# The sample group's bias in DRAM: twelve stores of shifted rows and six loads, in place of one store and 56 loads

## The chip, the cores and the metric

One Trainium2 chip, one core. The metric is the device time of one execution in microseconds (us). Engines are called PE (TensorE), DVE (VectorE), ACT (ScalarE), POOL (GpSimd) and SP (SyncE, which here only issues DMAs); ACT and POOL also issue some. L706 is line 706 of the kernel before.

## The reference

One inference step of one decoder layer, all in float32, for two groups of tokens that share the weights: a prompt of 2048 tokens, and a sample group of 8 sequences with 4 new tokens each and a cache of 1024 past positions. The input is normed and projected into three branches: attention over dilated windows (12 heads), a causal depthwise convolution, and cross-attention into 256 memory rows. What the change touches is the attention of the sample group: each head evaluates three patterns, and to each score a bias from a shared table is added that depends on head, pattern and distance.

```python
PATTERNS = ((128, 1), (512, 4), (2048, 16))   # window, dilation

def _dilated_gather(q, k_all, v_all, bias, d, nw, wb, past):
    i = jnp.arange(T)[:, None]
    j = jnp.arange(nw + 1)[None, :]
    kpos = past + i - j * d                    # keys at distances 0, d, .. nw*d
    ...
    s = jnp.einsum('bthd,btjhd->bthj', q, kg).astype(jnp.float32)
    s = s + bias.astype(jnp.float32)
    s = jnp.where(valid[None, :, None, :], s, NEG)
```

The four new tokens of a sequence stand one position apart, so along a row of cached keys the bias of token t is that of its neighbour, moved by one place.

## The kernel before, in words

The work stands in one long program. First (`phase_a1`) x is normed, transposed and split into a high and a low half, and multiplied with the columns of w_in block by block (u, q, k, v, qc); every float32 product is three matmuls, hi*hi, hi*lo and lo*hi (`gemm`, L166 to L168). The convolution of each u block follows on DVE. Then, in `build`, come `memory` (memory keys and values, the norm of the convolution's output, cross-attention), `sample_bias`, `sample_attention` and `attention`, and last `phase_c` with the output products. Beside memory and both attentions runs a generator of further column blocks (`sweep`: za, zb, zc, gt; tiles gg, weights whi and wlo), which gives TensorE work between the others.

The program's text isn't the order on the engines. The framework orders the instructions when the context closes, by a simulated timeline (`schedule_with_timeline_sim=True`): each engine and queue gets a list in which an instruction may move ahead of others that are not ready by that simulation. On the chip each engine then goes through its own list strictly in order. So loads of a later function can come early: those of `sample_bias` stand among those of `memory`.

The bias goes through DRAM:

- `bias_rows`, early in `phase_a1`, makes `exs`, 12 partitions (a head each) by 3 patterns by 752, with six small matmuls (L377) and six copies (L378) on DVE, and stores it to `d_exs` (L379). Row p of a head holds the negated bias over shifted positions: 515 places for the last 512 cached keys, 7 for the new ones, 4 x 32 for the older keys that only pattern 2 reaches, and one row's blocks are moved by 32 for a token.
- Behind it `blk_u` loads `st_in`, the old convolution rows (L275), which TensorE transposes (L279).
- `sample_bias` builds three tiles, one a pattern, of 112 rows: rows 0 to 47 and 64 to 111 are head times 4 plus token, twice. A memset fills a tile (L696, L698), then for each of the two halves and each of the four tokens one load brings 512 places (L706), one the 4 new places (L707), and for pattern 2 one the 128 older places (L709). Each load writes 12 partitions, four apart, from a place in `d_exs` that moves with the token. A copy (L710) repeats the new places eight times. That is 3 x 2 x 4 x 2 + 8 = 56 loads, all issued by SP.
- `sample_attention` reads the three tiles, some 400 us later, for its scores.

Other names that the prediction uses, all at the start of `memory`: `c` are chunks of the convolution's output (load L663), whose norm goes through DVE (L665, L668, L673, L685), ACT (sq, L671 and L684), POOL (L681) and two small matmuls (str L667, sco L675); `mt` are the memory rows (L913), `msq` their squares on ACT (L915), `mrs` and `mrr` the factors of their norm (L64 to L68); `wraw` from w_mem_kv are the memory weights (L150), which POOL splits into whi (L55) and wlo (L56).

Of the kernel before, what the change touches and what calls it, by code (L numbers as in the profile page):

```python
# [7 lines left out]
F32 = mybir.dt.float32  # L8
# [11 lines left out]
HA, DA, EA = 12, 64, 768  # L20
# [3 lines left out]
NT_S = 752  # L24
# [13 lines left out]
class K:  # L38
# [316 lines left out]
    def bias_rows(self, cpool, pool, psum):  # L355
        nc, I = self.nc, self.I
        rb = self.rb = cpool.tile([33, HA], F32, name="rb")
        nc.vector.memset(rb, 1.0e30)
        raw = pool.tile([32, HA], F32, name="rbr")
        nc.sync.dma_start(raw, I["rel_bias"])  # L360
        nc.vector.tensor_scalar(rb[0:32], raw, -1.0, None, op0=ALU.mult)
        oh = pool.tile([33, 3, 384], F32, name="oh")
        nc.sync.dma_start(oh, I["c_onehot"])
        ext = pool.tile([HA, 3, 384], F32, name="ext")
        for p in range(3):
            t = psum.tile([128, 512], F32, name="tr")
            nc.tensor.matmul(t[:HA, :384], rb, oh[:, p, :], start=True, stop=True)
            nc.vector.tensor_copy(ext[:, p, :], t[:HA, :384])
        nc.sync.dma_start(self.d_ext, ext)
        ohs = pool.tile([33, 3, NT_S], F32, name="ohs")  # L370
        nc.sync.dma_start(ohs, I["c_onehot_s"])
        exs = pool.tile([HA, 3, NT_S], F32, name="exs")
        for p in range(3):
            for c in range(0, NT_S, NT_S // 2):
                cs = slice(c, c + NT_S // 2)
                t = psum.tile([128, 512], F32, name="tr")
                nc.tensor.matmul(t[:HA, :NT_S // 2], rb, ohs[:, p, cs], start=True, stop=True)  # L377
                nc.vector.tensor_copy(exs[:, p, cs], t[:HA, :NT_S // 2])  # L378
        nc.sync.dma_start(self.d_exs, exs)  # L379
        pf = pool.tile([128, 3, 128], F32, name="permf")  # L380
        nc.sync.dma_start(pf, I["c_perm"])
        self.perm = cpool.tile([128, 3, 128], R32, name="perm")
        nc.vector.tensor_copy(self.perm, pf)
# [305 lines left out]
    def sample_bias(self, keep):  # L689

        nc = self.nc
        NK, R = 672, 112
        self.sbias = []
        for p in range(3):
            bt = keep.tile([R, NK], F32, name=f"sb{p}")
            nc.vector.memset(bt, 1.0e30 if p < 2 else 0.0)  # L696
            nw = keep.tile([R, 4], F32, name=f"sn{p}")
            nc.vector.memset(nw, 0.0)  # L698
            base = self.d_exs[:, p, :]
            for r in (0, 64):  # L700
                for t in range(4):
                    rows = slice(r + t, r + 48, 4)

                    def src(o, n):
                        return bass.AP(tensor=base.tensor, offset=base.offset + o, ap=[[base.ap[0][0], HA], [1, n]])
                    nc.sync.dma_start(bt[rows, 0:512], src(3 - t, 512))  # L706
                    nc.sync.dma_start(nw[rows, :], src(515 + 3 - t, 4))  # L707
                    if p == 2:
                        nc.sync.dma_start(bt[rows, 512:640], src(522 + 32 * (3 - t), 128))  # L709
            nc.vector.tensor_copy(bt[:, 640:NK].rearrange("p (b t) -> p b t", t=4), nw[:, None, :].to_broadcast([R, 8, 4]))  # L710
            self.sbias.append(bt)


    def sample_attention(self):
# [505 lines left out]
    def scratch(self, dp):  # L1220
        t = lambda n, sh: dp.tile(sh, F32, name=n)
        self.d_q = [t(f"d_q{j}", [128, T]) for j in range(6)]
        self.d_k = [t(f"d_k{j}", [128, T]) for j in range(6)]
        self.d_qc = [t(f"d_qc{j}", [128, T]) for j in range(4)]
        self.d_za = [t(f"d_za{j}", [128, T]) for j in range(6)]
        self.d_zb = [t(f"d_zb{j}", [128, T]) for j in range(6)]
        self.d_zc = [t(f"d_zc{j}", [128, T]) for j in range(4)]
        self.d_c = t("d_c", [6, 128, T])
        self.d_actb = t("d_actb", [6, 128, T])
        self.d_ext = t("d_ext", [HA, 3, 384])  # L1230
        self.d_exs = t("d_exs", [HA, 3, NT_S])
        self.d_st = [t(f"d_st{h}", [6, S]) for h in range(HA)]
        self.d_cf = [t(f"d_cf{j}", [3, 2 * S]) for j in range(6)]
        self.d_act = [None if 6 <= j < 12 else t(f"d_act{j}", [128, T]) for j in range(16)]
        self.d_act[6:12] = [self.d_actb[j] for j in range(6)]
        self.d_g = [t(f"d_g{j}", [128, T]) for j in range(24)]
        self.d_x = [None] + [[[t(f"d_x{th}{c}{k}", [128, THIRDS[th][1]]) for k in range(8)] for c in range(2)]
                             for th in (1, 2)]
# [69 lines left out]
```

## Time and profile before

| | before |
|---|---|
| median of 3 runs | 3151.36 us (3148.8 to 3155.62) |
| profiled execution | 3154.4 us |
| its span | 3152.6 us |
| PE busy | 3000.2 us, 95% of the span |
| DVE busy | 2014.8 us, 64% |
| POOL busy | 1350.4 us, 43% |
| ACT busy | 1124.2 us, 36% |
| DMA | 454.66 MB, mean 144 GB/s |
| chain that ended last | PE 70%, DMA 12%, DVE 7%, issue 4%, POOL 3%, ACT 2%, SP's queue 1% |

The profile is of one execution. Its busy times are sums over the span; a row of a timeline gives start, length, engine, line, operation, what is written from what, and in brackets how long the engine had idled before and what released it. A queue such as SPq only issues transfers: its rows are the time of the issue, and the transfer lands later. The chain follows each instruction back to what released it; "issue" in it is time without a wait that the profile shows.

### The profile page before, as it was taken

The numbers are of one execution on the slowest core, as the hardware profiler recorded it, in microseconds if no ns is written. First come the engines' busy times: TensorE is split into PE (matmuls) and PEld (weight loads), VectorE is DVE, ScalarE is ACT, GpSimd is POOL, SyncE is SP. The second block draws the span as 40 slices with busy tenths as digits, with TensorE's granted clock in tenths as the row PEclk, the third lists the DMA queues.
The fourth block names the chain that finished last, engine by engine and source line by source line (L and its number), as shares of the span: only waits on it lengthen the run. The fifth ranks groups of instructions, "written<-read, shape, count | busy, mean of one in ns | idle before, by whom it ended". The sixth has DMA issues, their size and how long they took to land.

```text
span 3152.6 us, 55374 instructions
## 1 busy us (share of the span) xinstructions
PE 3000.2 (95%) x20705; PEld 2839.9 (90%) x20705; DVE 2014.8 (64%) x3734; ACT 1124.2 (36%) x2835; POOL 1350.4 (43%) x1048
## 2 busy tenths in 40 slices
PE   7999999999987999999999999989899979999998
PEld 6899999999987999998999999989898967787897
DVE  5297797796677926465546766666656457556563
ACT  5010010010132433243437575656565523222221
POOL 0121221142356537444256565667676433233240
PEclk9899999999999999999999999999999989999999
DMA  7232222211265454477454656576555487657561
GB/s 250 85 103 80 80 60 61 63 62 50 81 182 167 135 153 144 147 219 239 151 139 116 161 123 163 128 185 150 156 143 152 109 279 227 223 168 227 161 197 53
DMA packets 532218, 454.66 MB, mean 144 GB/s; under 512 B 118191, under 2 KB 458581, under 8 KB 531137
## 3 DMA queue, kind: packets, MB, share of 16 engines
q1 hardware_dynamic: 357502, 335.36, 36.2%
q10 hardware_dynamic: 169840, 105.02, 11.7%
q0 software_dynamic: 4608, 10.75, 1.2%
q8 instruction: 164, 2.69, 0.4%
q14 instruction: 104, 0.85, 0.1%
HBM read 332.96 MB, written 118.04 MB: 143 GB/s over the span
## 4 chain that ended last, share of the span: by engine, by line
PE 70%; DMA 12%; DVE 7%; issue 4%; POOL 3%; ACT 2%; SPq 1%; ACTq 0%; DVEq 0%; POOLq 0%
PE g L166 8%; PE g L167 8%; PE g L168 8%; PE gg L166 6%; PE gg L168 6%; PE gg L167 6%; PE pg L168 3%; PE pg L166 3%; PE pg L167 3%; PE pt L571 2%; DMA cb<-d_cf 2%; PE y L1180 2%; PE y L1179 2%; PE y L1178 2%; PE o L598 1%
## 5 line engine op out<-in xcount | busy, mean ns | idle before, releaser
L166 PE MATMUL gg<-x0h,whi 128*128 128x256 f32 (+1 forms) x2560 | 747.9, 292 | 25.9 <-DVE st L246 12.2
L168 PE MATMUL gg<-x0h,wlo 128*128 128x256 f32 (+1 forms) x2560 | 741.8, 290 | 0.1
L167 PE MATMUL gg<-x0l,whi 128*128 128x256 f32 (+1 forms) x2560 | 741.1, 290 | 0.0
L55 POOL TENSOR_SCALAR whi<-wraw 128x1024 fp32r<-128x1024 f32 x162 | 242.7, 1500 | 928.5 <-PE g L167 524.1
L166 PEld LDWEIGHTS gg<-x0h,whi 128*128 128x128 f32 x2560 | 493.2, 193 | 35.0 <-DVE st L246 13.7
L167 PEld LDWEIGHTS gg<-x0l,whi 128*128 128x128 f32 x2560 | 493.5, 193 | 2.2 <-issue 0.5
L168 PEld LDWEIGHTS gg<-x0h,wlo 128*128 128x128 f32 x2560 | 493.2, 193 | 2.2 <-POOL wlo L56 0.3
L322 DVE SCALAR_TENSOR_TENSOR acc<-G,cw,acc 128x1536 f32<-128x1536 f32 (+15 forms) x354 | 480.8, 1408 | 0.3
L56 POOL TENSOR_TENSOR wlo<-wraw,whi 128x1024 fp32r<-128x1024 f32 x162 | 417.0, 2575 | 9.4 <-PE gg L168 0.2
L155 POOL TENSOR_TENSOR clo<-craw,chi 128x768 fp32r<-128x768 f32 (+1 forms) x96 | 174.1, 1815 | 346.0 <-ACT chi L154 329.8
L627 ACT ACTIVATE P<-T,stm 128x128 f32<-128x128 f32 (+1 forms) x576 | 260.8, 455 | 141.0 <-DVE stm L625 94.8
L239 ACT ACTIVATE st<-g 128x384 f32<-128x384 f32 (+1 forms) x132 | 60.2, 461 | 570.7 <-PE g L168 550.7
L166 PE MATMUL pg<-ac,chi 128*128 128x512 f32 (+1 forms) x640 | 229.4, 359 | 16.6 <-ACT chi L154 8.7
L625 DVE CUSTOM_DVE_ANT_0 T<-s,bias 128x128 f32<-128x128 f32 (+1 forms) x576 | 191.5, 357 | 80.8 <-PE s L617 47.0
L167 PE MATMUL pg<-ac,chi 128*128 128x512 f32 (+1 forms) x640 | 228.8, 358 | 6.3 <-DVE ac L1198 6.3
L168 PE MATMUL pg<-ac,clo 128*128 128x512 f32 (+1 forms) x640 | 227.6, 357 | 3.6 <-POOL clo L155 3.6
L576 DVE TENSOR_TENSOR pl<-pt,ph 128x512 fp32r<-128x512 f32 x240 | 155.6, 652 | 52.4 <-ACT ph L575 48.9
L168 PE MATMUL g<-x0h,wlo 128*128 128x384 f32 x544 | 184.3, 339 | 2.9 <-POOL wlo L56 2.9
L166 PE MATMUL g<-x0h,whi 128*128 128x384 f32 x544 | 183.6, 338 | 2.6 <-ACT st L239 2.3
L167 PE MATMUL g<-x1l,whi 128*128 128x384 f32 x544 | 186.0, 342 | 0.0
L167 PE MATMUL g<-x0l,whi 128*128 128x384 f32 x544 | 185.8, 342 | 0.0
L168 PE MATMUL g<-x1h,wlo 128*128 128x384 f32 x544 | 185.8, 342 | 0.0
(330 smaller groups left out, 7425.0 us busy)
## 6 DMA issues: line engine op xcount, KB each, us to landing
wraw<-in_w_in ACTq DMA_DIRECT2D x119, 512.0 KB
d_g<-st ACTq DMA_DIRECT2D x168, 128.0 KB
cb<-d_cf SPq DMA_DIRECT2D x72, 256.0 KB
g<-d_g SPq DMA_DIRECT2D x72, 256.0 KB
wraw<-in_w_in SPq DMA_DIRECT2D x35, 512.0 KB
kvc<-in_cache_k_win SPq DMA_DIRECT2D x8, 1536.0 KB
kvc<-in_cache_v_win SPq DMA_DIRECT2D x8, 1536.0 KB
raw<-d_q SPq DMA_DIRECT2D x48, 256.0 KB
```

Source lines behind the costliest of these rows:

```text
L55: nc.gpsimd.tensor_scalar(hi, raw, 1.0, 1.0, op0=ALU.mult, op1=ALU.mult)
L56: nc.gpsimd.tensor_sub(lo, raw, hi.bitcast(F32))
L155: nc.gpsimd.tensor_sub(lo, raw, hi.bitcast(F32))
L166: nc.tensor.matmul(ps, hi[:, k, :], h, start=k == 0, stop=False)
L167: nc.tensor.matmul(ps, hi[:, k, :], l, start=False, stop=False)
L168: nc.tensor.matmul(ps, lo[:, k, :], h, start=False, stop=k == kb - 1)
L322: nc.vector.scalar_tensor_tensor(a3[:, lo:hi], G[:, src:src + hi - lo, 2 - m:130 - m], w, a3[:, lo:hi], op0=ALU.mult, op1=ALU.add)
L571: nc.tensor.transpose(t[:, 128 * x:128 * x + 128], pc, self.ident)
L576: nc.vector.tensor_tensor(pl[:, :w], t[:, :w], ph[:, :w].bitcast(F32), op=ALU.subtract)
L625: nc.vector.tensor_tensor_reduce(sc[:, :w], t[:, o:o + w], bias[:, 256 - w:256], 1.0, 3.0e38, ALU.add, ALU.min, m)
L627: nc.scalar.activation(P[:, o:o + w], sc[:, :w], AF.Exp, bias=m, scale=-1.0, accum_out=self.stl[:, col:col + 1])
L1178: nc.tensor.matmul(y[:m, c, :], ah[:, ts_], bh[:, cs], start=k == 0, stop=False)
```

## The change

`d_exs` gets a row for each head and token: 12 x 4 x 3 x 644 in place of 12 x 3 x 752. `bias_rows` stores each token's shifted piece, three stores a token, twelve in all, the same `exs` being read at four offsets. `sample_bias` has one tile of 112 x 3 x 672 in place of three of 112 x 672; head and token together are now 48 neighbouring rows in DRAM, so that one load for each half brings the 512 places of all three patterns, one the 128 older places and one the new ones: six loads. Three memsets stand for six; the three copies of the new places stay, now behind all loads in the program's text.

```diff
-        nc.sync.dma_start(self.d_exs, exs)
+        for t in range(4):
+            nc.sync.dma_start(self.d_exs[:, t, :, 0:512], exs[:, :, 3 - t:515 - t])
+            nc.sync.dma_start(self.d_exs[:, t, :, 512:516], exs[:, :, 518 - t:522 - t])
+            nc.sync.dma_start(self.d_exs[:, t, 2, 516:644], exs[:, 2, 522 + 32 * (3 - t):650 + 32 * (3 - t)])
...
-        self.sbias = []
+        bt = keep.tile([R, 3, NK], F32, name="sb")
+        nc.vector.memset(bt[:, 0:2], 1.0e30)
+        nc.vector.memset(bt[:, 2], 0.0)
+        nw = keep.tile([R, 3, 4], F32, name="sn")
+        nc.vector.memset(nw, 0.0)
+        src = self.d_exs.rearrange("h t p x -> (h t) p x")
+        for r in (0, 64):
+            nc.sync.dma_start(bt[r:r + 48, :, 0:512], src[:, :, 0:512])
+            nc.sync.dma_start(bt[r:r + 48, 2, 512:640], src[:, 2, 516:644])
+            nc.sync.dma_start(nw[r:r + 48], src[:, :, 512:516])
         for p in range(3):
-            bt = keep.tile([R, NK], F32, name=f"sb{p}")
-            nc.vector.memset(bt, 1.0e30 if p < 2 else 0.0)
-            nw = keep.tile([R, 4], F32, name=f"sn{p}")
-            nc.vector.memset(nw, 0.0)
-            base = self.d_exs[:, p, :]
-            for r in (0, 64):
-                for t in range(4):
-                    ...
-            nc.vector.tensor_copy(bt[:, 640:NK].rearrange("p (b t) -> p b t", t=4), nw[:, None, :].to_broadcast([R, 8, 4]))
-            self.sbias.append(bt)
+            nc.vector.tensor_copy(bt[:, p, 640:NK].rearrange("p (b t) -> p b t", t=4),
+                                  nw[:, p, None, :].to_broadcast([R, 8, 4]))
+        self.sbias = [bt[:, p] for p in range(3)]
...
-        self.d_exs = t("d_exs", [HA, 3, NT_S])
+        self.d_exs = t("d_exs", [HA, 4, 3, 644])
```

More of the change, by code (lines that the diff above doesn't have):

```diff
@@ L692, in sample_bias @@
         NK, R = 672, 112
-        self.sbias = []
-        for p in range(3):
-            bt = keep.tile([R, NK], F32, name=f"sb{p}")
-            nc.vector.memset(bt, 1.0e30 if p < 2 else 0.0)
-            nw = keep.tile([R, 4], F32, name=f"sn{p}")
-            nc.vector.memset(nw, 0.0)
-            base = self.d_exs[:, p, :]
-            for r in (0, 64):
-                for t in range(4):
[L702 to L709, printed above, removed]
-            nc.vector.tensor_copy(bt[:, 640:NK].rearrange("p (b t) -> p b t", t=4), nw[:, None, :].to_broadcast([R, 8, 4]))
-            self.sbias.append(bt)
+        bt = keep.tile([R, 3, NK], F32, name="sb")
[8 more added lines that the diff above has]
+            nc.sync.dma_start(nw[r:r + 48], src[:, :, 512:516])
+        for p in range(3):
+            nc.vector.tensor_copy(bt[:, p, 640:NK].rearrange("p (b t) -> p b t", t=4),
+                                  nw[:, p, None, :].to_broadcast([R, 8, 4]))
+        self.sbias = [bt[:, p] for p in range(3)]
     def sample_attention(self):
```

## The prediction

> **What bounds the kernel now.** I read the page first, then busy time by stretch, then the rows of the tensor that the change touches, then the queues and engines around them in order of time, and last the chain of waits there.
>
> ```profile
> span 3152.6 us, 55374 instructions
> PE 3000.2 (95%) x20705; PEld 2839.9 (90%) x20705; DVE 2014.8 (64%) x3734; ACT 1124.2 (36%) x2835; POOL 1350.4 (43%) x1048
> ```
>
> TensorE (PE) is busy for 3000.2 of 3152.6 us and has the same matmuls in both kernels. So the change can win only what TensorE idles beside it, 152.4 us in the whole span, and lose what it adds to that. The next view is the tensor d_exs, which alone is laid out anew (three numbers after the count: shortest, median, longest in ns; then the first and the last start).
>
> ```profile
> L706 SPq DMA_DIRECT2D sb<-d_exs x24: 690/700/2790, 870.7 to 928.0; - x24
> L707 SPq DMA_DIRECT2D sn<-d_exs x24: 691/700/888, 872.7 to 928.8; - x24
> L709 SPq DMA_DIRECT2D sb<-d_exs x8: 690/700/1829, 909.0 to 929.5; - x8
> L379 SPq DMA_DIRECT2D d_exs<-exs x1: 324/324/324, 112.8 to 112.8; - x1
> ```
>
> The 56 loads (24 + 24 + 8) hold SP's queue from 870.7 to about 930 us; the one store stands at 112.8. Those are the two places to look at. Busy time by stretch (the columns: length, busy time with the number of instructions for PE, weight loads, VectorE, ScalarE, GpSimd; then granted clock, DMA share, GB/s):
>
> ```profile
> core 0: us, PE busy (x) PEld busy (x) DVE busy (x) ACT busy (x) POOL busy (x), PEclk, DMA share, GB/s
> 870.00:930.00 60.00, 48.22 (x345) 45.60 (x344) 47.35 (x54) 20.76 (x35) 25.79 (x20) 0.89 0.66 198
> 930.00:1000.00 70.00, 55.57 (x419) 53.66 (x417) 52.23 (x36) 17.50 (x26) 47.52 (x45) 0.90 0.44 130
> ...
> 870.00:880.00 10.00, 8.23 (x66) 7.80 (x64) 5.84 (x6) 0.77 (x2) 0.00 (x0) 1.00 0.93 315
> 890.00:900.00 10.00, 8.18 (x43) 7.95 (x42) 9.73 (x11) 2.13 (x4) 8.86 (x5) 0.67 0.37 101
> ```
>
> While the loads are issued TensorE idles 60 - 48.22 = 11.8 us: the most that their removal can win directly. In the 70 us after them it idles 14.4 us, with none of them left. And from 870 to 880 us the DMA engines are 93% busy at 315 GB/s: there bytes are the limit, not SP.
>
> **The change part by part.** *The six loads in place of 56.* SP's queue in order of time (start, length, line; below it one row that groups all loads of c, and one wait: total, times, longest):
>
> ```profile
> 869.57 1.07 SPq L663 DMA_DIRECT2D c<-d_c  x2
> 870.72 0.82 SPq L706 DMA_DIRECT2D sb<-d_exs  x1
> ...
> 872.68 0.75 SPq L707 DMA_DIRECT2D sn<-d_exs  x1
> 873.48 1.02 SPq L913 DMA_DIRECT2D mt<-in_mem_prompt  x2
> 875.06 0.73 SPq L706 DMA_DIRECT2D sb<-d_exs  x1
> ...
> 880.76 1.31 SPq L150 DMA_DIRECT2D wraw<-in_w_mem_kv  x2
> ...
> L663 SPq DMA_DIRECT2D c<-d_c x9: 360/371/624, 866.4 to 1075.8; - x9
> SPq L707 <- DMA c<-d_c: 1.2, 1, 1.2
> ```
>
> Removed: 56 issues of 0.70 us, 0.74 with the gap behind each (the chain below has one at 880.02 and the next instruction at 880.76), 41 us of SP. Added: six issues. No load of 48 rows by three runs is in the trace; bounds are 0.37 us (c, many rows of several runs each) and 0.70 us (the loads removed, whose 12 rows lie four partitions apart). The new rows lie next to each other as those of c do, so I take 0.37, with a gap of 0.08 (869.57 + 1.07 to 870.72) 0.45 each and 2.7 us in all. SP gains 39 us. The bytes stay: 2 x 48 x 3 rows of 2 KB are 590 KB, as the 24 loads of 12 rows were.
>
> What of that reaches TensorE? Not the sum, but the few issues that stand in front of something awaited. Ahead of mt (the memory rows) stand one sb and one sn, 0.82 + 0.75 us. If the first two new loads take their places, that is 0.90, so mt is issued 0.67 us sooner; but 295 + 25 KB now go before it through full DMA engines in place of 25 KB: 0.94 us more at the row's 315 GB/s. Net, mt lands 0.3 us later. Those who wait for mt:
>
> ```profile
> 880.84 1.06 ACT L915 ACTIVATE msq<-mt 128x1024 f32<-128x1024 f32 x1 [4.94 <-DMA sb<-d_exs]
> 883.39 2.84 DVE L673 TENSOR_REDUCE sm<-sq 128x256 f32<-128x1536 f32 x1 [5.98 <-ACT sq L671]
> 886.28 1.22 PE L675 MATMUL sco<-sm,ones 128*128 128x256 f32 x2 [1.27 <-DVE sm L673]
> ```
>
> ScalarE idles 4.94 us before msq, which reads mt; sq of the convolution's norm stands behind it, then VectorE's sum, then TensorE's in-order queue. The name sb in that wait is the landing that came last by the profile; msq reads only mt. So this term is +0.3 us, between -0.7 (issue alone counts) and +2.0 (all 644 KB of the new loads go ahead of mt).
>
> Next comes wraw, the first memory weights. The wait of 1.2 us for c stays; behind it four more new issues at 0.45 take the place of five old ones at 0.74, so wraw is issued some 2 us sooner, with about 0.3 MB (1 us) more ahead of it in the engines: it lands 1 us sooner. The chain of waits goes through here:
>
> ```profile
> 870.01 7.03 DMA c<-d_c
> 877.05 0.70 SPq L707
> ...
> 880.02 0.70 SPq L707
> 880.76 0.51 SPq L150
> 881.69 8.63 DMA wraw<-in_w_mem_kv
> 890.34 0.70 SPq L707
> ...
> 891.83 1.93 DMA sn<-d_exs
> ...
> ```
>
> The chain goes on from sn's landing (893.76) to VectorE's reciprocal lnr at 894.17. I don't follow it there:
>
> ```profile
> 891.86 7.01 POOL L56 TENSOR_TENSOR wlo<-wraw,whi 128x1024 fp32r<-128x1024 f32 x3
> 891.94 2.31 DVE L66 TENSOR_TENSOR mrs<-mrs,mss 128x2 f32<-128x2 f32 x1
> 894.17 1.74 DVE L64 RECIPROCAL lnr<-lns 128x256 f32<-128x256 f32 x1
> ...
> 908.89 3.57 DVE L685 SCALAR_TENSOR_TENSOR c<-sq,c 128x1536 f32<-128x1536 f32 x1 [0.95 <-ACT sq L684]
> ...
> 938.52 12.59 DVE L685 SCALAR_TENSOR_TENSOR c<-sq,c 128x1536 f32<-128x1536 f32 x1 [2.60 <-ACT sq L684]
> ```
>
> The reciprocal doesn't read the bias, and VectorE had a product of 128x2 elements in hand until 894.25, held up for the length of one GpSimd wlo (7.01 / 3 = 2.34 us). So VectorE was busy, not waiting for sn. I count wraw's earlier landing at -0.5 us (between 0 and -1) and sn at 0; if the chain is right, that is a rival below. Between 890 and 930 us the loads delay only what others have slack for (the later c, the stores of k), since none of the stretch's TensorE gaps that I saw ended on a DMA that SP issued: 0. The three memsets write the elements that six wrote, and the three copies of sn come one after another: 0, hidden in VectorE's 12.7 us of idle time (60 - 47.35); if a copy comes up before its load has landed, VectorE stands behind it, at most for a landing of 1.93 us.
>
> *Twelve stores in place of one.* SP, TensorE and TensorE's queue near the store:
>
> ```profile
> 112.81 0.32 SPq L379 DMA_DIRECT2D d_exs<-exs  x1
> 113.23 6.91 SPq L275 DMA_DIRECT2D st_in<-in_state_conv  x2
> ...
> 134.34 0.39 SPq L150 DMA_DIRECT2D wraw<-in_w_in  x1
> ...
> 119.41 0.37 PE L279 MATMUL tr<-ident,st_in 120*128 120x120 f32 x2
> ...
> L279 PEldq EVENT_SEMAPHORE  x5: 51/51/51, 116.3 to 588.9; - x5
> ```
>
> Behind the store SP loads st_in, the old convolution rows, which TensorE transposes at 119.41 in the middle of the first u block. The queue passed that wait at 116.3, in 51 ns. With the shortest landing above, st_in landed near 113.23 + 0.34 + 1.93 = 115.5: 3.9 us of slack. Eleven more issues ahead of it cost 11 x 0.42 (113.23 - 112.81, issue and gap of the one store) = 4.6 us, or 11 x 0.74 = 8.1 us if they go at the pace of the loads of 12 rows. TensorE would then stand 0.7 or 4.2 us; nothing if the ordering puts st_in ahead of stores or the transposes later. Stores read 12 neighbouring partitions as L379 does, so I take +0.7. Nobody else is near: SP has nothing else to issue until 134 us, and the bias is read 750 us later.
>
> *Sum.* +0.3 - 0.5 + 0.7 = +0.5 us. The profiled execution took 3154.4 us for a span of 3152.6, 3 us above the median of the runs, 3151.36. The forecast is for the median: 3151.4 + 0.5, rounded 3152 us. The runs lie between 3148.8 and 3155.6, so about 0.2% (6.3 us) is what can be told from no change.
>
> **Two rules of the Trainium skill.** The row of the 56 loads beside TensorE's 48.22 of 60 busy us says 11.8 us at most. The Trainium skill, "DMA: Bandwidth & Descriptors" (Rules for kernel authors, and Anatomy of one DMA), says to join small transfers and gives about 2.0 us fixed per DMA, for the GpSimd path; 50 fewer would be 100 us if they stood in line, and by it the time would be 3051 us. The trace disagrees that they stand in line: they were issued 0.74 us apart.
>
> The row of the 128x2 product beside wlo is the other place. The Trainium skill, "SBUF — State Buffer" (on the shared port pair), says that a VectorE instruction with two SBUF inputs and a GpSimd one that reads SBUF exclude each other for a whole instruction. The trace agrees (2.31 us beside 2.34), and the last rival follows from it.
>
> **The rivals.** *The chain is right:* SP's bias issues and sn's landing release TensorE. Then 877.05 to 880.76 (3.7 us) and 890.34 to 893.76 (3.4 us) fall away: 7.1 us, 3144 us. For it: the chain. Against: VectorE's rows.
>
> *All of the idle time is SP's:* 11.8 us, and with the gaps the low clock (8.18 us of work at 0.67 in 890 to 900, 2.7 us): 3137 us. Against: the next stretch idles as much without any bias load. A change that brings nothing because the ordering drags the loads elsewhere is in my own case.
>
> *Slower: st_in comes late.* At 0.74 us a store TensorE stands 4.2 us, and the low clock behind such a gap adds 2.7: +6.9, 3158 us. It starts at 3.9 / 11 = 0.35 us a store, and passes 6.3 us only from 0.7 on, and if the transposes keep their place. For it: slack of only 3.9 us. Against: L379's 0.32.
>
> *Another VectorE instruction is caught by GpSimd.* L685 took 3.57 us free and 12.59 behind a run of GpSimd splits, 9.0 us, just after the loads. Weights that land 1 us sooner move those splits. It can go either way: 3143 or 3161 us.
>
> **How the numbers follow.** My case 0.60 (its own range 3146 to 3157); the chain is right 0.15; all idle time 0.03; st_in late 0.09; caught by GpSimd 0.06 faster and 0.07 slower. Faster by over 0.2%: most of the 0.15, 0.03, 0.06 and a tail of my case, 0.22; slower: two thirds of 0.09, 0.07 and a tail, 0.15; same 0.63. The range is 3141 to 3160: it takes in the chain's rival and the late st_in and leaves out the whole idle time and about half of the caught cases.
>
> **What would show it.** Six loads at about 0.4 us and SP idle between 880 and 930; msq starting near 881; TensorE idle in 870 to 930 near 12 us still; twelve stores 0.42 us apart from about 112.8, st_in issued near 117.8 and TensorE's gap before L279 under 1 us. Wrong would be: a gap of over 3 us at L279; idle time under 5 us in 870 to 930 (the chain's rival); or a L685 near 12 us that was short, or the other way round.

## The result and the profile after

The changed kernel takes 3177.18 us (median of 6 runs, 3171.86 to 3185.35), before 3150.08 us (6 runs, 3141.57 to 3155.62): a ratio of 1.0082 with a 95% interval of 1.0066 to 1.0097, 27 us slower. The forecast was 3152 us, with 3160 as its upper end. The profiled execution of after took 3185.35 us, 8 us above its median, that of before 3154.4, so of the 31 us between the two spans some 4 belong to these two executions and not to the change.

The head of the page of after:

```profile
span 3183.6 us, 55342 instructions
PE 3011.7 (95%) x20705; PEld 2847.3 (89%) x20705; DVE 2029.2 (64%) x3731; ACT 1120.9 (35%) x2835; POOL 1346.5 (42%) x1048
```

The same 20705 matmuls. The tensor d_exs, one row a line of code:

```profile
L381 SPq DMA_DIRECT2D d_exs<-exs x4: 340/364/364, 114.0 to 117.6; - x4
...
L704 SPq DMA_DIRECT2D sb<-d_exs x2: 537/596/654, 871.4 to 879.2; - x2
L705 SPq DMA_DIRECT2D sb<-d_exs x2: 340/464/587, 874.3 to 880.9; - x2
L706 SPq DMA_DIRECT2D sn<-d_exs x2: 543/564/585, 875.7 to 881.3; - x2
```

The parts did what they say: twelve short stores, six loads of 0.34 to 0.65 us, all issued by 882 us. Busy time by stretch, after, with the columns of the prediction; the last row is the longer stretch in which the convolution's norm runs:

```profile
870.00:930.00 60.00, 37.47 (x267) 34.02 (x267) 45.11 (x49) 18.02 (x30) 22.11 (x18) 0.80 0.67 187
...
880.00:890.00 10.00, 2.62 (x13) 1.73 (x12) 5.88 (x7) 5.12 (x7) 0.00 (x0) 0.69 1.10 255
890.00:900.00 10.00, 2.51 (x6) 1.20 (x5) 9.39 (x11) 2.23 (x4) 9.81 (x7) 0.50 0.55 163
900.00:910.00 10.00, 5.35 (x33) 4.98 (x34) 8.14 (x8) 1.13 (x3) 6.55 (x7) 0.61 0.29 87
...
866.40:1145.00 278.60, 226.35 (x1718) 217.56 (x1717) 222.22 (x272) 96.26 (x179) 143.99 (x133) 0.91 0.52 153
```

and before, two of the short stretches and that last one:

```profile
880.00:890.00 10.00, 3.25 (x10) 1.91 (x8) 6.45 (x6) 5.50 (x8) 4.60 (x4) 0.67 0.83 244
...
900.00:910.00 10.00, 10.00 (x85) 10.00 (x84) 6.66 (x12) 4.15 (x8) 5.82 (x8) 0.98 0.67 191
...
866.40:1145.00 278.60, 241.84 (x1866) 233.38 (x1865) 208.39 (x276) 101.36 (x188) 156.00 (x142) 0.95 0.53 162
```

From 870 to 930 us TensorE idles 22.5 us instead of 11.8, at a granted clock of 0.80 instead of 0.89, and is 78 matmuls behind (345 to 267). By 1145 us it is 148 behind (1866 to 1718), about 17.8 us at the 0.12 us from one gg row to the next: nearly half of that falls behind 930 us, where neither kernel has any bias left to load. The largest wait of TensorE that is new by 1145 us is one for mt, the normed memory rows (waits of TensorE from 866 to 1145 us: in all, times, longest; after, then before):

```profile
PE gg L166 <- DVE st L246: 14.6, 8, 8.9
...
PE tr L923 <- DVE mt L919: 7.9, 1, 7.9
```

```profile
PE gg L166 <- DVE st L246: 10.1, 9, 1.8
```

And VectorE, with four instructions fewer, is busy 13.8 us longer. The norm ends as much later; its last sum on TensorE in before, then in after:

```profile
1127.39 0.30 PE L675 MATMUL sco<-sm,ones 128*128 128x32 f32 x2
```

```profile
1141.15 0.30 PE L679 MATMUL sco<-sm,ones 128*128 128x32 f32 x2
```

Where VectorE's 13.8 us lie is told by its groups in the same stretch, one row a line and shape (busy us, mean ns of one). Before:

```profile
L685 DVE SCALAR_TENSOR_TENSOR c<-sq,c 128x1536 f32<-128x1536 f32 x8 | 35.0, 4372 | 19.3 <-ACT sq L684 19.3
...
L64 DVE RECIPROCAL lnr<-lns 128x256 f32<-128x256 f32 x8 | 13.9, 1743 | 4.0 <-ACT lns L63 4.0
...
L65 DVE TENSOR_TENSOR lns<-lnr 128x256 f32<-128x256 f32 x8 | 6.3, 785 | 0.0
L66 DVE TENSOR_TENSOR lns<-lns,var 128x256 f32<-128x256 f32 x8 | 5.1, 643 | 0.1
...
L68 DVE TENSOR_TENSOR lnr<-lns,lnr 128x256 f32<-128x256 f32 x8 | 3.4, 421 | 0.1
...
L67 DVE TENSOR_SCALAR lns<-lns 128x256 f32<-128x256 f32 x8 | 2.3, 287 | 0.1
```

After:

```profile
L689 DVE SCALAR_TENSOR_TENSOR c<-sq,c 128x1536 f32<-128x1536 f32 x8 | 35.5, 4436 | 13.2 <-ACT sq L688 13.2
...
L64 DVE RECIPROCAL lnr<-lns 128x256 f32<-128x256 f32 x8 | 13.9, 1744 | 4.8 <-ACT lns L63 4.8
...
L65 DVE TENSOR_TENSOR lns<-lnr 128x256 f32<-128x256 f32 x8 | 9.7, 1214 | 0.0
...
L66 DVE TENSOR_TENSOR lns<-lns,var 128x256 f32<-128x256 f32 x8 | 8.2, 1029 | 0.1
...
L68 DVE TENSOR_TENSOR lnr<-lns,lnr 128x256 f32<-128x256 f32 x8 | 7.1, 887 | 0.1
L67 DVE TENSOR_SCALAR lns<-lns 128x256 f32<-128x256 f32 x8 | 5.3, 659 | 0.1
```

The 32 small instructions of L65 to L68 take 6.3 + 5.1 + 3.4 + 2.3 = 17.1 us before and 9.7 + 8.2 + 7.1 + 5.3 = 30.3 us after: 13.2 us more, nearly the whole difference (the others nearly cancel). They stand one behind the other in each of the norm's chunks, and their work is the same. What lengthens them is seen at 934 us of after; VectorE, then GpSimd:

```profile
932.15 1.72 DVE L65 TENSOR_TENSOR lns<-lnr 128x256 f32<-128x256 f32 x1
933.91 2.51 DVE L66 TENSOR_TENSOR lns<-lns,var 128x256 f32<-128x256 f32 x1
```

```profile
931.20 4.95 POOL L56 TENSOR_TENSOR wlo<-wraw,whi 128x1024 fp32r<-128x1024 f32 x2
```

L65 ends at 933.87, as the first of the two subtractions wlo does by half of 4.95 us (933.68), and L66 at 936.42, behind the second (936.15); each would take 0.41 us alone. In before 3 of the 32 take over 0.7 us, in after 13; all of these run beside an instruction of GpSimd, 3 and 8 of them beside a wlo. So after meets GpSimd's instructions more often. The wait of 7.9 us for mt comes about in part in the same way: between 895.86 and 904.60 us four VectorE instructions, the last of them the one that writes mt, are lengthened beside three wlo and a whi.

Not all of the loss lies here. Of the 31 us between the spans, 19.5 are more idle time of TensorE (171.9 us instead of 152.4), and 15.5 of these fall before the end of cross-attention (52.3 us idle from 866.9 to 1328.2 us after, 36.8 from 866.4 to 1312.9 before); 4.8 fall into attention. The other 11.5 us are the same matmuls taking longer, at a granted clock of 0.94 instead of 0.97 up to the end of cross-attention, and 0.97 instead of 0.98 in attention. So somewhat over half of the difference arises in the memory stage; what comes later was not followed.

### The profile page after: what moved, and what is told of

Read it like the earlier page. It is cut to its first block, busy times and chain, and to the rows that moved or that the text cites. A ratio compares the mean times of both kernels' runs of the same rounds, so it can differ in the third digit from the quotient of the medians.

```text
span 3183.6 us, 55342 instructions
## 1 busy us (share of the span) xinstructions
PE 3011.7 (95%) x20705; PEld 2847.3 (89%) x20705; DVE 2029.2 (64%) x3731; ACT 1120.9 (35%) x2835; POOL 1346.5 (42%) x1048
## 5 line engine op out<-in xcount | busy, mean ns | idle before, releaser
L166 PE MATMUL g<-x1h,whi 128*128 128x384 f32 x544 | 182.4, 339 | 0.0
```

The lines of the kernel that those rows point to most:

```text
L166: nc.tensor.matmul(ps, hi[:, k, :], h, start=k == 0, stop=False)
```

## The experiments

Times are medians, ratios are to runs of before that were taken beside them (before: 3150 to 3151 us each time); code that is left out is marked by three dots. "The list" is the order in which the built program's instructions stand on an engine; it was read from the built programs. gg is the filler between the other work, so the number of gg rows ahead of a marker tells how the plan was remade. Ahead of the first and the last transpose of mt, and of the first product of cross-attention, before has 132, 227 and 627, after 76, 144 and 528.

### First: stores, bytes, SP's issues

**e1_stores.** The twelve stores and the new layout, with 56 loads from it.

```diff
-            nc.sync.dma_start(bt[r:r + 48, :, 0:512], src[:, :, 0:512])
...
+            for r in (0, 64):
+                for t in range(4):
...
+                    nc.sync.dma_start(bt[rows, 0:512], self.d_exs[:, t, p, 0:512])
...
```

> The changed layout and its twelve stores, but the bias loaded from it by 56 loads of 12 rows as before, in the old places. In this kernel's list for TensorE 58 rows of the filler gg stand between the first sum over the convolution's norm (sco) and the first transpose of the memory rows, as in before (after: 4). Theory 'order' (the planner, whose lists follow a simulated timeline, brings the memory rows' transposes ahead of gg once SP's queue is free): 3150 us, TensorE's idle time in 870 to 930 us near 12 us. Theory 'bytes' (the two loads of 295 KB in one piece go ahead of mt and the weights through full DMA engines): 3150 us too. Rival 'stores' (the twelve stores or the new layout in DRAM cost it): a good part of the 27 us stays, over 3160 us. It clears or charges the first half of the change alone.

3149.20 us, ratio 0.9996 (0.9982 to 1.0010); ahead of the three markers the list has as many rows as in before. The stores and the layout cost nothing; the loss is in the loads.

**e3_nobig.** After without the two loads of the 512 places.

```diff
-            nc.sync.dma_start(bt[r:r + 48, :, 0:512], src[:, :, 0:512])
```

> After without its two loads of 48 x 3 rows of 2 KB (590 KB); the bias of the 512 cached places is left out of the computation, the four small loads stay. The written order stays that of after (4 rows of gg between sco and the first transpose of mt, both gg weights not ahead of msq). Theory 'order': about 3175 us, the wait for the first memory-row transpose stays near 8 us and TensorE idles about 22 us in 870 to 930. Theory 'bytes': mt lands about 2 us and the weights about 2 us sooner, and the time falls to about 3155 us. In between (about 3165) would say that both have a half.

3164.49 us, 1.0042 (1.0019 to 1.0064): in between, and the runs lie far apart (3148.57 to 3177.92). The trace has 76 and 144 rows of gg ahead of the first and the last transpose, as in after, and the wait for mt is 7.9 us again. So with the order of after and no bytes to speak of some 13 us stay, by the medians.

**e8_dummy50.** 50 tiny loads more on SP.

```diff
...
+            for x in range(25):
+                nc.sync.dma_start(dm[r + x % 4:r + 48:4, x, :], self.d_exs[:, x % 4, 0, 512:516])
```

> After with 50 tiny loads more (12 rows of 16 bytes each, 10 KB in all, into a tile that nobody reads) behind the six on SP's queue, so SP has its old number of issues again, and the six large loads are still in one piece ahead of mt. The planner's list then has 48 rows of gg between sco and the first transpose of mt. Theory 'order': it goes back to about 3150 to 3156 us, although it issues 50 loads more and moves as many bytes. Theory 'bytes': it stays at 3177 us or above. A prediction that SP's issues cost TensorE time would have it slower than after.

3173.19 us, 1.0058 (1.0039 to 1.0077). The list has 120 rows ahead of the first transpose, close to before, and the loss stays: against theory "order", with "bytes".

**e2_late.** The six loads about 100 us later.

```diff
...   (mark[7]: the last store of the memory values)
-                        self.sample_bias(sk)
+                        with tc.issue_after(self.mark[7].ins):
+                            self.sample_bias(sk)
```

> After with the six loads placed behind the last store of the memory values (out_v_mem), some 100 us later, where nothing of the memory rows waits for DMA. SP then issues mt at once and the four memory weights right behind, still ahead of ScalarE's two gg weights. The planner's list has 26 rows of gg between sco and the first transpose of mt. Theory 'bytes': the whole loss goes, about 3150 us or less. Theory 'order': about 32/54 of the loss stays, near 3166 us. Theory 'weights' (the memory weights land ahead of the filler's weights, because SP is free): about 3177 us, as in after.

3172.16 us, 1.0055 (1.0037 to 1.0073): against "bytes", since none of the bias goes ahead of mt. It also shows a meeting that after doesn't have. The copies of the new places now meet GpSimd; VectorE, then GpSimd:

```profile
1009.81 8.64 DVE L708 COPY sb<-sn 112x32 f32<-112x32 f32 x1 [4.86 <-DMA cq<-d_qc]
```

```profile
1009.12 3.50 POOL L1016 MEMSET xqz<- 128x4096 f32 x1
```

The three copies take 0.18 us each in after. An instruction of the norm (L689) is held over the same 8.5 us, so the copies' own share of the loss can't be told from this. After these four no theory stood: TensorE's order and the bytes were each spoken for by one run and against by another.

### Second: TensorE's order alone, both ways

**pin_all.** After, with TensorE's list held to the filler of before.

```diff
...
+            for m, n in self.pins:   # m: instruction of the memory stage, n: rows of gg ahead of it in before
+                tc.add_manual_dep(m.ins, self.gg[n - 1].ins.name, NOSYNC, reason="pin")   # NOSYNC: order alone, no wait
```

> After with one thing more: edges of order alone (no wait) in TensorE's list, which hold the memory rows' transposes, the products of the memory weights and the two sums of the convolution's norm behind as many rows of gg as in before's list. The list then has 132 rows of gg ahead of the first transpose of mt (before 132, after 76), 234 ahead of the last (227, 144) and 627 ahead of the first product of cross-attention (627, 528). SP's list is that of after: six loads in one piece ahead of mt, the memory weights four in a row. Theory 'plan' (the loss is filler that the planner no longer sets ahead of work that the chip can't have ready): 3147 to 3155 us, TensorE's idle time in 870 to 930 near 12 us. Rival 'bytes' (the burst of 640 KB delays mt and the filler's weights): 3165 to 3177. Rival 'weights' (SP being free lets the memory weights go ahead of the filler's): near 3172, as e2_late.

3176.08 us, 1.0067 (1.0042 to 1.0092): no gain. Its waits of TensorE (in all, times, longest) show one reason:

```profile
PE gg L167 <- DVE st L249: 31.9, 10, 9.9
PE gg L167 <- POOL whi L56: 13.2, 1, 13.2
```

The filler stands ahead of the memory rows again, but waits 13.2 us for its own weights, so this run isn't a clean test of the order.

**before_pinned.** Before, with rows of gg held behind the same markers.

```diff
...
+            for m, n in self.pins:
+                tc.add_manual_dep(self.gg[n].ins, m.ins.name, NOSYNC, reason="pin")
```

> Before with its 56 loads in their old layout, and edges of order alone that hold rows of gg behind the markers of the memory stage, as after's list has them. The list comes out with somewhat less filler than after's: 77 rows of gg ahead of the first transpose of mt (before 132, after 76), 142 ahead of the last (227, 144), 448 ahead of the first product of cross-attention (627, 528). Nothing of the change is in it. Theory 'plan': as slow as after or slower, 3172 to 3195 us. Rivals 'bytes' and 'weights', and 'stores': no reason for a loss, 3145 to 3156.

3150.67 us, 0.9993 (0.9979 to 1.0008), with about as little filler ahead of mt as after and less ahead of cross-attention. TensorE waits 6.6 us for mt here too and loses nothing by the end. Theory "plan" in the sense of TensorE's order falls: its order isn't enough for the loss. That it isn't needed either rests on e8_dummy50, which has close to before's filler ahead of the first transpose and loses 22 us.

**e4_before_late.** Before with its 56 loads where e2_late has six.

```diff
...
-                        self.sample_bias(sk)
+                        with tc.issue_after(self.mark[7].ins):
+                            self.sample_bias(sk)
```

> Before with its 56 loads behind the last store of the memory values, some 100 us later. SP is free in the memory stage, as in after, and no bias load stands ahead of mt or the weights. The planner sets 98 rows of gg ahead of the first transpose of mt and 186 ahead of the last (before 132 and 227). Theory 'plan': about the time of e2_late, 3165 to 3175 us, though it has none of the new layout, stores or joined loads. A prediction by SP's issues (they stand in TensorE's way) has it at 3140 to 3150.

3158.84 us, 1.0025 (1.0007 to 1.0043): slower, though the issues are out of the way and nothing of the change is in it; between the two forecasts. It is 13 us less than e2_late, with the same filler ahead of the markers.

**w_pool.** After, the memory weights issued by GpSimd.

```diff
-            w = self.load_w(wp, I["w_mem_kv"][0, :, 128 * c:128 * c + 128], 8)
+            w = self.load_w(wp, I["w_mem_kv"][0, :, 128 * c:128 * c + 128], 8, q=nc.gpsimd)
```

> After with the eight loads of the memory weights issued by GpSimd instead of SP. In the planner's timeline they come later, and it sets 109 rows of gg ahead of the first transpose of mt, 189 ahead of the last and 624 ahead of the first product of cross-attention (after 76, 144, 528; before 132, 227, 627). Theory 'plan': most of the loss goes, 3150 to 3162 us, unless GpSimd's issues, which stand in order with its splits, delay the weights. Rival 'bytes': 3170 or more, since the burst ahead of mt stays. Rival 'weights': the memory weights no longer go ahead of the filler's, 3150 to 3160 too.

3149.36 us, 0.9989 (0.9975 to 1.0004): the whole loss is gone, with the burst still ahead of mt. Its row:

```profile
866.40:1145.00 278.60, 245.32 (x1902) 236.56 (x1901) 203.09 (x273) 103.27 (x192) 163.18 (x150) 0.96 0.54 162
```

VectorE is busy 19.1 us less than in after (222.22 - 203.09). That is where the theory "caught" comes from: that the norm's chunks pace the stage, and that their VectorE instructions are lengthened by GpSimd's subtractions.

### Third: the subtractions

**mtfirst.** After, the six loads behind mt.

```diff
...
+                        with tc.issue_after(self.mark.ins):   # the second load of mt
                             self.sample_bias(sk)
```

> After with its six loads placed behind the second load of mt on SP's queue, so that none of their 640 KB goes ahead of the memory rows. Theory 'caught' (the pace of the memory stage is set by the nine chunks of the convolution's norm, whose instructions on VectorE are held up whenever they meet a subtraction wlo on GpSimd; the change only re-dealt these meetings): the first chunk ends (store d_actb) some 3 to 5 us sooner than in after's 917.8, the later ones at their own pace, 3155 to 3177 us, and the time goes with the summed lengthening of VectorE's instructions in the stage (before 49 us at 3151, after 63 at 3177). Theory 'bytes' (the burst ahead of mt is all of it): 3148 to 3156.

3170.22 us, 1.0057 (1.0033 to 1.0082): "bytes", in the sense of a burst ahead of mt, falls. msq, the first reader of mt, still starts late here, at 885.20 us; but it starts at 886.56 in w_pool, which loses nothing, and at 879.27 in mid3 below, which loses 19 us, so the delay of mt isn't the loss either. The first chunk is stored at 915.52 us instead of 917.84, as expected. VectorE is as long as in after:

```profile
866.40:1145.00 278.60, 230.77 (x1740) 222.49 (x1740) 220.38 (x273) 98.66 (x182) 152.85 (x139) 0.90 0.52 153
```

**b_wpool.** Before with w_pool's edit.

> Before with its eight loads of the memory weights issued by GpSimd, the control for w_pool (after with the same, 3149 us). If that edit gains by itself some 25 us, this kernel takes about 3125 us and the change costs as much with it as without. If the change's loss hangs on the order of this stage alone (theory 'caught'), there is no reason for such a gain: 3140 to 3160 us, and w_pool stands within 10 us of it.

3153.45 us, 1.0002 (0.9988 to 1.0015): the edit gains nothing by itself. On the changed kernel it takes away what the change brought.

**vlo** and **b_vlo.** In after and in before, the subtraction of these weights on VectorE.

```diff
...
-        nc.gpsimd.tensor_sub(lo, raw, hi.bitcast(F32))
+        (nc.vector if vec else nc.gpsimd).tensor_sub(lo, raw, hi.bitcast(F32))
```

> After with the subtraction wlo of the filler's and the memory weights done by VectorE instead of GpSimd, in both kernels of this pair. Theory 'caught': VectorE's instructions in the memory stage are no longer lengthened by it (63 us in after, under 25 here), and the loss against the same edit of before shrinks from 27 us to under 10. In absolute time VectorE takes over some 120 subtractions of 1024 elements, about 1.1 to 1.3 us each by its products of that width, so the time itself may go either way, 3130 to 3190 us. Theory 'bytes': the pair still differs by 20 us or more.

> Before with the same subtraction on VectorE, the control for the run above. Theory 'caught': within 10 us of it. Theory 'bytes': 20 us or more faster than it. Its own lengthening on VectorE falls from 49 us to under 25.

vlo 3161.11 us, 1.0028 (1.0013 to 1.0044); b_vlo 3155.30 us, 1.0004 (0.9988 to 1.0019). The loss shrinks from 27 us to 5.8 by the medians; the intervals overlap. The edit remakes the lists of both kernels as well (115 and 127 rows ahead of the first transpose instead of 76 and 132). Summed over VectorE's rows from 866 to 1145 us, what is above the shortest of the same operation in any of these traces is 50 us in before and 64 in after (49 and 63 when the expectations were written, with fewer traces), 31 in b_vlo and 27 in vlo: a little more than the 25 expected.

**b_twice.** Before, the filler's subtraction twice.

```diff
...
+            if again:
+                nc.gpsimd.tensor_sub(lo, raw, hi.bitcast(F32))
```

> Before, with the subtraction wlo of the filler's weights done a second time by GpSimd, the same numbers into the same tile, for the first third of the columns: some 39 more instructions of 2.4 us on an engine that was busy 249 of 450 us in this stage. Theory 'caught': the summed lengthening of VectorE's instructions from 866 to 1145 us rises from 50 us to 65 or more, the last norm sum comes at 1140 or later instead of 1127, and the time is 3165 to 3190 us, without any part of the change. Theory 'weights on SP': 3148 to 3158 us. If TensorE's waits for wlo grow by over 5 us, the test isn't clean.

3198.07 us, 1.0166 (1.0126 to 1.0206): 48 us slower, more than expected, with nothing of the change. Of the 39 further subtractions 16 have started by 1145 us, and by then TensorE is 259 matmuls behind before. The last norm sum comes at 1161.18 us, and the lengthening is 73 us. The list is remade here too (100 rows ahead of the first transpose instead of 132). Its row, and the waits that answer the proviso:

```profile
866.40:1145.00 278.60, 222.61 (x1607) 213.49 (x1606) 225.98 (x261) 91.05 (x168) 176.35 (x140) 0.88 0.47 143
```

```profile
PE gg L168 <- DVE st L248: 31.9, 9, 11.1
...
PE gg L170 <- POOL wlo L159: 2.1, 1, 2.1
```

TensorE waits 2.1 us for the later wlo, but 31.9 us for VectorE's st, the emptying of the filler's results (before: 10.1 by the same view). That is how VectorE's time becomes TensorE's here: the filler can't go on while st stands in VectorE's queue. In after itself this wait grew less, from 10.1 to 14.6 us; the rest is the wait for mt and smaller ones.

### Fourth: the queue of the weights

**mid3.** After, the six loads behind the fourth memory weight on SP.

```diff
...
+                        with tc.issue_after(self.mark.ins):   # the load of the fourth memory weight
                             self.sample_bias(sk)
```

> After with the six loads placed behind the fourth of the memory weights on SP's queue, about 902 us, so nothing of them goes ahead of mt or of the first weights. Theory 'weights on SP': SP still issues the memory weights four in a row from 874 us, 3158 to 3175 us. Theory 'caught': the time goes with the lengthening of VectorE's instructions, whichever it is: at 50 us near 3155, at 63 near 3175. Theory 'bytes' would have 3150.

3169.31 us, 1.0061 (1.0037 to 1.0086), and a lengthening of 55 us: inside the range of "weights on SP", against "bytes", and some 7 us above what "caught" gives for 55 us (between 3155 at 50 and 3175 at 63).

**e7_actw.** w_pool with ScalarE's queue (q=nc.scalar).

> After with the memory weights issued by ScalarE instead of SP. SP is as free as in w_pool (3149 us), the burst stays ahead of mt, and the list sets only 103 rows of gg ahead of the last transpose of mt and 443 ahead of the first product of cross-attention (after 144 and 528). Theory 'weights on SP': 3148 to 3158 us. Theory 'caught': by the lengthening of VectorE's instructions, as above, whatever queue issues the weights. Theory 'plan' (less filler ahead), if anything of it is left: over 3180.

3170.88 us, 1.0068 (1.0047 to 1.0089). Against "weights on SP". It fits "caught" badly too: the lengthening is 51 us, hardly above before. It has the least filler of all ahead of the last transpose (103 rows), so what it loses may be that; no run shows it.

**mtfirst_wpool.** The two edits together.

> After with the six loads behind mt and the memory weights issued by GpSimd, the two edits that the runs point to. Theory 'weights on SP': 3145 to 3155 us, as w_pool or a little better, since the burst is no longer ahead of mt. Theory 'caught': near 3150 if the lengthening of VectorE's instructions is under 50 us.

3156.03 us, 1.0023 (1.0005 to 1.0041): just above both forecasts and no better than w_pool, though its lengthening is the smallest of all with the subtractions on GpSimd, 40 us. No version beat before by more than its interval.

### All of them together

One profiled execution a kernel, from 866.4 to 1145 us. "Norm rows" are VectorE's time on the tile lns and on c<-sq,c (in before 32.2 + 35.0), gg the rows ahead of the last transpose of mt. vlo and b_vlo are left out, since VectorE does other work in them. In b_twice the norm is so late that only 7 of its 8 large chunks are counted.

| kernel | time, median | VectorE | TensorE | norm rows | gg |
|---|---|---|---|---|---|
| e1_stores | 3149.2 | 208.7 | 243.4 | 66.4 | 227 |
| w_pool | 3149.4 | 203.1 | 245.3 | 59.2 | 189 |
| before_pinned | 3150.7 | 204.5 | 239.1 | 58.0 | 142 |
| before | 3151.4 | 208.4 | 241.8 | 67.2 | 227 |
| b_wpool | 3153.5 | 208.6 | 240.2 | 65.5 | 206 |
| mtfirst_wpool | 3156.0 | 199.8 | 242.2 | 59.8 | 187 |
| e4_before_late | 3158.8 | 210.0 | 238.0 | 66.0 | 186 |
| e3_nobig | 3164.5 (profiled 3155.7) | 208.2 | 239.9 | 59.8 | 144 |
| mid3 | 3169.3 | 214.6 | 234.6 | 70.5 | 186 |
| mtfirst | 3170.2 | 220.4 | 230.8 | 77.3 | 159 |
| e7_actw | 3170.9 | 210.5 | 233.9 | 69.0 | 103 |
| e2_late | 3172.2 | 213.7 | 227.9 | 73.3 | 186 |
| e8_dummy50 | 3173.2 (profiled 3159.9) | 219.6 | 234.9 | 69.6 | 192 |
| pin_all | 3176.1 | 215.2 | 226.4 | 69.8 | 234 |
| after | 3177.2 | 222.2 | 226.4 | 80.9 | 144 |
| b_twice | 3198.1 | 226.0 | 222.6 | 81.4 | 172 |

Up to 67.2 us of norm rows the kernels take 3149 to 3165 us, from 69.0 us on 3169 to 3198. The line was drawn after the runs and is thin: from before (67.2 us) to e7_actw (69.0) the time rises by 19.5 us, from before_pinned (58.0) to before by 0.7. The last norm sum on TensorE parts the same kernels more clearly: it starts at 1118 to 1129 us in the eight faster ones and at 1133 to 1161 in the others. The last column has no such line. Nor do the 32 small instructions alone: they take 30.3 us in after, but 27.0 in e3_nobig, 21.8 in w_pool and 17.2 in mid3.

What is shown: somewhat over half of the profiled difference arises in the memory stage; the kernels that lose 19 us or more are those whose norm ends late; more subtractions on GpSimd bring such a loss (b_twice), and most of it goes away where GpSimd doesn't do them (vlo beside b_vlo). That the meetings with GpSimd are the cause of the 27 us is argued from this, since every one of these edits remade the lists as well. What stays open: why the new lists meet the subtractions more often, and what the loss behind the memory stage is. Several edits that leave SP free in this stage lost 8 to 27 us, e8_dummy50 lost 22 with SP as full as before, and among the edits of transfers only moving the weights to GpSimd's queue undid it; no run isolates a single move in VectorE's or GpSimd's list.

## Why the prediction was wrong, point by point

- **The step that failed:** the sum, +0.3 - 0.5 + 0.7, over the transfers that someone waits for, in an order taken as given. SP's 39 us were seen, and that they don't reach TensorE directly was right. But the planner orders every engine's list by a simulated timeline, SP's issues are in that timeline, and with 50 fewer the lists came out otherwise far beyond the loads (76 rows of gg ahead of mt instead of 132). "Between 890 and 930 us the loads delay only what others have slack for ... : 0" has no term for that, nor for what VectorE and GpSimd do to each other in another order. The term stood at 0, and the loads' part of the change took 27 us, with 15.5 us more idle time of TensorE by the end of cross-attention.
- **VectorE and GpSimd.** The last rival named the mechanism, with 0.13 over both signs, and priced one meeting: 9.0 us, for L685 with 12.59 us. That one neither went nor grew (after has an L689 of 12.20 us at 945.47, the same instruction). What grew was 32 small instructions by 13.2 us together; had the rival been priced by the stretch instead of by one instruction, its slower side could have stood near 3152 + 13 = 3165 us. That c<-sq,c has 35.0 us in 8 where 8 x 1.76 = 14 would do, and that these rows stand one behind the other in every chunk, could be read in the profile before.
- **mt, +0.3 (bounds -0.7 to +2.0).** msq starts at 885.77 us instead of 880.84, beyond the upper end. Here the rows of after on SP and ScalarE:

```profile
873.34 0.91 SPq L912 DMA_DIRECT2D mt<-in_mem_prompt  x2
...
879.22 0.54 SPq L704 DMA_DIRECT2D sb<-d_exs  x1
```

```profile
882.60 1.48 ACT L675 ACTIVATE sq<-c 128x1536 f32<-128x1536 f32 x1 [5.02 <-DMA mt<-in_mem_prompt]
...
885.77 1.06 ACT L914 ACTIVATE msq<-mt 128x1024 f32<-128x1024 f32 x1 [1.68 <-DMA sb<-d_exs]
```

  Two things were mis-sized. The bytes: mt was issued 873.48 - 873.34 = 0.14 us sooner, yet ScalarE's load of the filler's weights, which in both built lists waits for the landing of an mt (SP and ScalarE share eight completion semaphores in rotation), goes out at 882.12 instead of 878.89 us. So the first mt landed some 3.2 us later, where the term had 0.94 us for the bias ahead of it at 315 GB/s. And the order, for the other 1.7 us: on ScalarE the norm's sq now goes ahead of msq, and behind it a store that waits for the landing of a bias load (the sb in the row), by the same rotation. With the six loads behind mt (mtfirst) msq starts at 885.20 us, no sooner to speak of, because another load of the filler's weights ahead of it waits for a bias load in that way; with no bias near mt at 880.65 (e2_late) and 879.61 (e4_before_late). So the burst holds msq up by some 5 us in either place. "msq reads only mt" was true and beside the point, since what a queue waits for first is the instruction ahead; the name sb in the row of before was such a wait.
- **wraw, -0.5.** Issued at 881.86 instead of 880.76 us: the second half of the bias waited for landings ahead of it (issued at 879.22, 3.6 us behind the load before it, 3.0 of them a wait for a c), so the new issues weren't 0.45 us each in a row.
- **The stores, +0.7 with a rival at 3158.** Right in mechanism: 0.41 us apart from 113.99, st_in issued at 118.88 us, 4.9 us behind the first store (5.0 predicted). TensorE didn't wait at L279, because the plan set it 30 matmuls later, as the prediction allowed; e1_stores confirms it as 0.
- **What would show it:** TensorE idle near 12 us in 870 to 930 was 22.5; the gap before L279 was none, as said; SP had four memory weights to issue from 882 to 902 us and stood at them, 11.5 us of it in waits that a wlo of GpSimd ended; and the L685 of 12.59 us has its like in after, with 12.20 us.
- **The two rules.** The Trainium skill, "DMA: Bandwidth & Descriptors" (Rules for kernel authors), says to join small transfers. 56 joined into six made this kernel slower as it was ordered, and w_pool, with the same six, is as fast as before. The Trainium skill, "SBUF — State Buffer" (on the shared port pair), says that a VectorE instruction with two SBUF inputs and a GpSimd one that reads SBUF exclude each other, and so do one in a mode that uses both ports and any GpSimd one. The trace agrees: L65, L66 and L68, with two inputs, are lengthened, L67 as well, and the reciprocal L64, 13.9 us for 8 in both kernels, never.

## What to carry to other kernels

Where a planner orders the lists, removing issues from a queue that nobody waits for need not be free: compare the built lists of all engines before costing the transfers, and look for the chain that paces the stage rather than for the engine that is busiest. Read groups by shape and compare the mean of one with its shortest: instructions at two to three times their own length in a chain show time that a new order can spend or save. A change of 0.2 to 1% in such a kernel should be tried in two or three orders (here one edit to another queue) before it is called a gain or a loss.

## What the runs showed of the hardware that was not expected

- In e2_late one of VectorE's small copies, 0.18 us long in after, took 8.64 us, from 1009.81 to 1018.45. For the first 2.8 us of it only a memset ran on GpSimd (1009.12 to 1012.62), which has no input; another memset and splits followed, and it ended with the last of them, a wlo.
- In b_twice 39 more subtractions of 2.4 us, 16 of them by 1145 us on an engine that had been busy 156 of 279 us, went with a loss of 48 us, though TensorE waited only 2.1 us for their results in that stretch.
